# Two gate products ahead of the retention branch, instead of one, in a hybrid retention and gated-linear-attention layer

## The chip, the cores and the metric

The kernel runs on one core of a Trainium2 chip. The metric is the device time of one execution in microseconds (us). A core has a matrix engine (TensorE, in the profile PE for matmuls and PEld for weight loads), VectorE (DVE), ScalarE (ACT), GpSimd (POOL), SyncE (SP, which here only issues DMAs), and 16 DMA engines.

## What is computed

One decoder layer over 528 positions (16 meta tokens ahead of 512 tokens), model width 1024, in float32. One input projection gives the parts of two branches and two merge gates. Cut to what matters here:

```python
u = rms_norm(h, norm_gain)
(rq, rk, rv, rg, gq, gk, gv, gg, glr, m_ret, m_gla) = jnp.split(u @ w_in, points, axis=-1)
o_ret = head_group_norm(retention_chunked(rope(rq), rope(rk) * 256 ** -0.5, rv), ret_norm_gain) * silu(rg)   # 4 heads: 256 q/k, 512 v
o_gla = head_rms_norm(gla_chunked(gq * 128 ** -0.5, gk, gv, log_a), gla_norm_gain) * silu(gg)                # 4 heads: 128 q/k, 256 v
merged = sigmoid(m_ret) * (o_ret @ w_branch_ret) + sigmoid(m_gla) * (o_gla @ w_branch_gla)
out = rms_norm(h + merged @ w_out, final_norm_gain)[:, 16:]
```

The change touches the stage in which `sigmoid(m_gla)`, the gate of the linear-attention branch, is computed beside `o_ret @ w_branch_ret` of a single retention head.

## The kernel before

**Numbers in two parts.** Every float32 operand of a large matmul is split into a high part (a rounded copy made by ScalarE) and a low part (the difference, made by VectorE): `split`, line 153, recorded at line 154. A product is then three matmuls: high by high, low by high, high by low.

**The quad.** A block of a projection (512 columns) is computed by `quad` (line 257) as seven products instead of eight, with sums of weight blocks on VectorE and sums of input blocks prepared beforehand. Its seven products are separated by `yield`. Each product (line 307) is 24 matmuls of 128x256, recorded at line 318. Before its matmuls come the split of its weights (line 302) and, for some, a sum of weight blocks (lines 355, 356, 371, 377). In the gate quad (`adds=False`) four raw weight tiles are loaded by SyncE (line 288); the fifth, x3, is a tile that VectorE fills at line 355 as the second product's step begins. After products come evacuations: a copy on ScalarE (line 334), a sum on VectorE (line 823), and for the gates a scaling on VectorE (line 1137) and a sigmoid on ScalarE (line 1138).

**The gate of linear attention.** `gates_gla(j)` (line 1362) loads what an earlier stage kept in DRAM (tile kg), runs a quad named mg for 512 columns of `m_gla`, multiplies the kept values by the gate (line 1374) and writes them back through GpSimd's queue (line 1131). Its PSUM tiles are mg_a, mg_b and mg_c, its weights mg_w (raw), mg_h and mg_l (parts).

**The retention branch of one head.** `branch` (line 463), called by `ret_branch(h)` (line 1406), multiplies the head's turned output (oh and ol, high and low) by its rows of `w_branch_ret`. It has eight steps, one for each 128 output columns: 12 matmuls of 128x512 (lines 189, 192, 193, in `mm3`), a copy out of PSUM by ScalarE (line 1409, tile mt), and a DMA from GpSimd that adds it to a DRAM tile (line 1131). Steps 1, 3, 5 and 7 first load and split a weight block (br_w, br_h, br_l).

**What the branch needs first.** `ret_attention(h)` ends with `turn` (line 478): transposes on TensorE (line 484, tile ot), then oh on ScalarE (line 491) and ol on VectorE (line 492), eight of each for a head. This runs between the products of the next head's q/k quad (rqk).

**Buffers.** Raw weight tiles share six buffers, weight parts three for high and three for low (`wsplit`, line 251). The temporary tiles of rope, scores and mt share seven. Quads and branches use PSUM pools of four banks each.

**What sets the order.** The program is written as generators. `weave(dense, chain, skip)` (line 204) takes a step of the dense generator, then, from the skip-th on, a step of the chain. `turns` (line 1172) takes one step of each of its generators in rotation until all have ended. TensorE's large products keep the order in which they are written, since the first matmul of each is made to follow the last of the one before (`pin`, line 183). The other engines' queues are put in order by the framework's planner, from its own estimates, when the kernel is built; at run time each engine works through its queue. The loop at line 1443 goes over the four heads. For heads h = 1 and 2 (line 1449) its middle stage is line 1450: the gate quad and the branch of head h - 1 in turns, with rope of head h (`ret_rope`, line 1242) as the chain. Then follow the head's output gate (quad rg) with the scores, and the values (quad rv).

Of the kernel before, what the change touches and what calls it, by code (L numbers as in the profile page):

```python
# [108 lines left out]
def hybrid_kernel(ctx: ExitStack, tc: tile.TileContext, I, out: bass.AP):  # L109
# [43 lines left out]
    def split(hi, lo, src):  # L153
        return nc.scalar.copy(hi, src), nc.vector.tensor_sub(lo, src, hi.bitcast(F32))  # L154
# [49 lines left out]
    def weave(dense, chain, skip=0):  # L204

        for n, _ in enumerate(dense):
            tick()
            if n >= skip:
                next(chain, None)
        for _ in chain:  # L210
            pass

    def every(gen, n, m=1, other=None):

        for i, _ in enumerate(gen):
            yield
            if i % m == m - 1:
                for _ in range(n - m):
                    if other is not None:
                        next(other, None)  # L220
                    yield

    def run(*gens):
        for g in gens:
            yield from g

    def drain(*gens):
        for g in gens:
            for _ in g:
                tick()  # L230
# [4 lines left out]
    def tick():  # L235

        pend[:] = [(n - 1, f) for n, f in pend]
        while pend and pend[0][0] <= 0:
            pend.pop(0)[1]()
# [223 lines left out]
    def branch(src, row0, oh, ol, name, evac, bank=ppt):  # L463
        for q in range(4):
            raw = wraw(f"{name}_{q}_w")
            hi, lo = wsplit([P, 4, 256], f"{name}_{q}")
            nc.sync.dma_start(raw, src[row0:row0 + 4 * P, q * 256:(q + 1) * 256].rearrange("(k p) c -> p k c", p=P))
            split(hi, lo, raw)
            for cc in range(2):
                c = 2 * q + cc  # L470
                ps = bank(f"{name}_p{c}")
                for k in range(4):
                    mm3(ps, hi[:, k, cc * P:(cc + 1) * P], lo[:, k, cc * P:(cc + 1) * P], oh[:, k, :], ol[:, k, :],
                        k == 0, k == 3, True)
                evac(c, ps)
                yield
# [126 lines left out]
    for q in range(4):  # L603
        raw = graw[q]
        hi, lo = wsplit([P, 2, 512], f"gv0_{q}")
        for kk in range(2):
            kh, k = divmod(2 * q + kk, 4)
            g = ng[:, 2 * q + kk:2 * q + kk + 1]
# [520 lines left out]
    def collect(dst, t, first):  # L1129

        nc.gpsimd.dma_start(dst, t, **({} if first else {"accum_op": ALU.add}))


    def gate(dst, p, q, th, n):
        if q is not None:
            total(dst, p, q)
        nc.vector.tensor_mul(dst, p if q is None else dst, rb[:, th, :256].unsqueeze(1).to_broadcast([P, 2, 256]))
        nc.scalar.activation(dst, dst, AF.Sigmoid, scale=(1.0, -1.0)[n])
# [33 lines left out]
    def turns(*gens):  # L1172
        gens = list(gens)
        while gens:
            for g in list(gens):
                try:
                    next(g)
                    yield
                except StopIteration:
                    gens.remove(g)  # L1180
# [21 lines left out]
    def tmp(name):  # L1202
        return rp.tile([P, 2 * HT], F32, tag="tmp", name=name, bufs=7)[:, :512]
# [4 lines left out]
    def rope(t, c, name, prev=None):  # L1208

        def view(m):  # L1210
            return m[:, :t.shape[2] * t.shape[3]].rearrange("p (h c) -> p h c", h=2)

        m = [view(rp.tile([P, 2 * HT], F32, tag="tmp", name=f"{name}_{i}", bufs=7)) for i in range(4)]
        x = nc.vector.tensor_mul(m[0], t[:, 0], c[0])
        if prev is not None:
            after(x, prev)
            after(nc.vector.tensor_mul(m[1], t[:, 1], c[1]), prev)
        else:
            nc.vector.tensor_mul(m[1], t[:, 1], c[1])
        nc.vector.tensor_sub(m[0], m[0], m[1])  # L1220
        yield
        nc.vector.tensor_mul(m[2], t[:, 1], c[0])
        nc.vector.tensor_mul(m[3], t[:, 0], c[1])
        nc.vector.tensor_add(m[2], m[2], m[3])
        yield
        R[name] = m[0], m[2]

    def ret_qk(h):

        q = rp.tile([P, 2, 2, 256], F32, tag="ql", name=f"q{h}")  # L1230
        k = rp.tile([P, 2, 2, HT], F32, tag="kl", name=f"k{h}")
        R["raw", h] = q, k

        def evac(n, th, x, y):
            d = q[:, :, th] if n else k[:, :, th]
            for t in range(2):
                w = d.shape[2]
                total(d[:, t], x[t][:, :w], y if y is None else y[:, t, :w])

        yield from quad((C_RK + h * 256, C_RQ + h * 256), False, f"rqk{h}", evac, wide=True)  # L1240

    def ret_rope(h):
        q, k = R["raw", h]
        yield from rope(k, (cs[:, 0], cs[:, 1]), f"rpk{h}", None if h % 3 else low[1])
        kh = rp.tile([P, 2, 2, HT], F32R, tag="kh", name=f"kh{h}")
        kl = rp.tile([P, 2, 2, HT], F32R, tag="kl", name=f"kl{h}")
        for i, m in enumerate(R[f"rpk{h}"]):
            split(kh[:, i], kl[:, i], m)
        for r in range(4):
            nc.gpsimd.tensor_copy(km[:, :, 32 * r:32 * r + NM].rearrange("p k (h m) -> p k h m", h=2),  # L1250
                                  (kh if r < 3 else kl)[:, :, :, 256:HT].bitcast(F32))
        yield
        yield from rope(q, (cs[:, 0, :, :256], cs[:, 1, :, :256]), f"rpq{h}")
        qh = rp.tile([P, 2, T], F32R, tag="qh", name=f"qh{h}")
        ql = rp.tile([P, 2, T], F32R, tag="ql", name=f"ql{h}")
        R["qk", h] = qh, ql, kh, kl
        for i, m in enumerate(R[f"rpq{h}"]):
            split(qh[:, i].rearrange("p (h c) -> p h c", h=2), ql[:, i].rearrange("p (h c) -> p h c", h=2), m)
        yield

    def ret_g(h):
        sg = rp.tile([P, NTB, 512], F32, tag="sg", name=f"sg{h}")
        R["sg", h] = sg
        yield from quad((C_RG + h * 512, C_RG + h * 512 + 256), True, f"rg{h}", rows_into(sg, AF.Silu),
                        ahead=h % 3 == 0, behind=R.get(("pow", h - 1)))
# [96 lines left out]
    def gates_gla(j):  # L1362

        c = slice(4 * j, 4 * j + 4)
        g = rp.tile([P, 4, T], F32, tag="vl", name=f"mg{j}")
        k = rp.tile([P, 4, T], F32, tag="vh", name=f"kg{j}")
        nc.sync.dma_start(k, kept[:, c, :])

        def evac(n, th, p, q):
            s = slice(2 * n, 2 * n + 2), slice(th * 256, (th + 1) * 256)  # L1370
            gate(g[:, s[0], s[1]], p, q, th, n)

            def later():
                nc.vector.tensor_mul(k[:, s[0], s[1]], k[:, s[0], s[1]], g[:, s[0], s[1]])
                collect(kept[:, c, :][:, s[0], s[1]], k[:, s[0], s[1]], True)

            pend.append((1, later))

        yield from quad((C_MG + j * 512, C_MG + j * 512 + 256), False, f"mg{j}", evac, adds=False)
# [26 lines left out]
    def ret_branch(h):  # L1406
        def evac(c, ps):
            t = tmp(f"mt{h}{c}")
            nc.scalar.copy(t, ps)
            collect(kept2[:, c, :], t, h == 0)  # L1410

        oh, ol = R["o", h]
        yield from branch(I["w_branch_ret"], h * 512, oh, ol, f"br{h}", evac, pat)
# [29 lines left out]
    for h in range(4):  # L1443
        if h == 0:
            drain(ret_qk(h))
        else:
            at = ret_attention(h - 1)
            weave(ret_qk(h), at if h < 3 else islice(at, NTB + 1))
        if h % 3:
            weave(turns(gates_gla(h - 1), ret_branch(h - 1)), ret_rope(h), skip=2)  # L1450
            weave(ret_g(h), ret_scores(h))
            drain(ret_v(h))
        else:
            weave(run(ret_g(h), ret_v(h)), run(every(ret_rope(h), 3, 2, at if h else None), ret_scores(h)))
# [153 lines left out]
```

## Time and profile before

| what | us |
|---|---|
| runs | 764.01, 763.93, 763.68 |
| median | 763.93 |
| profiled execution, span from first to last instruction | 762.2 |
| TensorE busy | 750.4 (98%) |
| VectorE busy | 611.2 (80%) |
| ScalarE busy | 451.2 (59%) |
| GpSimd busy | 133.4 (17%) |

The profile is one execution. Its page has no time beside the span; the runs' median is 1.75 us above it. Times of rows are counted from the span's start. A row of the timeline gives start and duration in us, engine, line, operation, output<-inputs, shapes and a count, and in brackets the idle time of the engine before it with what ended that. "L492" is line 492 of the kernel. Durations of matmuls overlap, since they are pipelined.

### The profile page before, as it was taken

The page shows a single profiled execution, that of the slowest core. Times are in us where ns is not written, and L with a number is a line of the kernel's source. Part 1 is how long each engine was busy: PE and PEld are TensorE (multiplying, and loading weights), DVE is VectorE, ACT ScalarE, POOL GpSimd, SP SyncE. Part 2 cuts the span into 40 slices and gives each one's busy share as a digit, 9 for nine tenths or more (in the row PEclk, how much of TensorE's full clock was granted, in tenths as well). Part 3 has the DMA queues.
Part 4 walks back from the last instruction along what each step waited for, and adds up shares of the span by engine and source line. Part 5 has one row for each costly group of instructions (what it writes and reads, how often), then busy time and mean ns, then how long its engine had stood idle before and what let it go on. Part 6 is the DMA issues. An engine that isn't in the chain of part 4 may idle for free.

```text
span 762.2 us, 14057 instructions
## 1 busy us (share of the span) xinstructions
PE 750.4 (98%) x5595; PEld 701.5 (92%) x5595; DVE 611.2 (80%) x873; ACT 451.2 (59%) x764; POOL 133.4 (17%) x172
## 2 busy tenths in 40 slices
PE   9999999999989999999999999999999999999996
PEld 6799899999989999998889999889999999988996
DVE  6799877689897799778957688876787989775994
ACT  7897584666974465545646455555554756532562
POOL 2211200112231122110330100240002210111142
PEclk9999999999999999999999999999999999999999
DMA  9864321822568973753684563696477357687503
GB/s 301 277 146 106 89 84 45 185 82 70 137 168 229 295 171 91 164 144 119 176 239 125 117 161 111 166 206 154 120 166 159 93 148 193 227 196 199 136 29 111
DMA packets 99995, 116.89 MB, mean 153 GB/s; under 512 B 5717, under 2 KB 90837, under 8 KB 99673
## 3 DMA queue, kind: packets, MB, share of 16 engines
q1 hardware_dynamic: 79896, 88.19, 37.8%
q0 software_dynamic: 19744, 27.27, 19.6%
q8 instruction: 44, 0.72, 0.4%
q10 hardware_dynamic: 288, 0.53, 0.2%
q14 instruction: 23, 0.18, 0.1%
HBM read 104.44 MB, written 11.53 MB: 152 GB/s over the span
## 4 chain that ended last, share of the span: by engine, by line
PE 87%; DVE 9%; issue 2%; ACT 1%; POOL 0%; POOLq 0%; DVEq 0%
PE rv_b L318 6%; PE rg_b L318 6%; PE rqk_b L318 5%; PE rqk_c L318 4%; PE br_p L192 4%; PE br_p L193 3%; PE br_p L189 3%; PE gg_b L318 3%; PE mr_b L318 3%; PE gv_p L640 3%; PE rv_c L318 3%; PE bg_b L318 3%; PE rg_c L318 3%; PE mg_b L318 2%; PE gg_c L318 2%
## 5 line engine op out<-in xcount | busy, mean ns | idle before, releaser
L192 PE MATMUL br_p<-ol,br_h 128*128 128x512 f32 x128 | 50.6, 395 | 1.7 <-DVE ol L492 1.7
L189 PE MATMUL br_p<-oh,br_h 128*128 128x512 f32 x128 | 50.4, 394 | 0.0
L193 PE MATMUL br_p<-oh,br_l 128*128 128x512 f32 x128 | 50.3, 393 | 0.0
L154 ACT CAST rv_h<-rv_w 128x1024 fp32r<-128x1024 f32 x24 | 25.2, 1052 | 26.9 <-DVE rv_w L371 9.6
L154 DVE TENSOR_TENSOR rv_l<-rv_w,rv_h 128x1024 fp32r<-128x1024 f32 x24 | 29.3, 1221 | 9.2 <-ACT rv_h L154 9.2
L154 DVE TENSOR_TENSOR rg_l<-rg_w,rg_h 128x1024 fp32r<-128x1024 f32 x20 | 24.4, 1219 | 8.4 <-ACT rg_h L154 8.4
L192 PEld LDWEIGHTS br_p<-ol,br_h 128*128 128x128 f32 x128 | 24.0, 188 | 7.4 <-DVE ol L492 2.4
L154 ACT CAST br_h<-br_w 128x1024 fp32r<-128x1024 f32 x16 | 16.8, 1050 | 23.4 <-PE br_p L192 9.9
L282 POOL DMA_DIRECT2D rqk_x<-in_w_in_dram x8 | 10.4, 1305 | 109.5 <-DVE vl L154 66.2
L193 PEld LDWEIGHTS br_p<-oh,br_l 128*128 128x128 f32 x128 | 24.0, 188 | 5.5
L154 ACT CAST rg_h<-rg_w 128x1024 fp32r<-128x1024 f32 x20 | 21.0, 1052 | 13.2 <-PE br_p L192 5.0
L189 PEld LDWEIGHTS br_p<-oh,br_h 128*128 128x128 f32 x128 | 24.0, 188 | 5.1 <-ACT oh L491 0.2
L318 PE MATMUL rv_b<-rv_l,fh 128*128 128x256 f32 x96 | 27.1, 282 | 0.1
L318 PE MATMUL rqk_b<-fh,rqk_h 128*128 128x256 f32 (+1 forms) x96 | 27.2, 283 | 0.0
L318 PE MATMUL rqk_b<-fh,rqk_l 128*128 128x256 f32 (+1 forms) x96 | 27.1, 282 | 0.0
L318 PE MATMUL rqk_b<-fl,rqk_h 128*128 128x256 f32 (+1 forms) x96 | 27.1, 282 | 0.0
L154 DVE TENSOR_TENSOR rqk_l<-rqk_w,rqk_h 128x1024 fp32r<-128x1024 f32 x20 | 24.4, 1220 | 3.3 <-ACT rqk_h L154 3.3
L318 PE MATMUL rg_b<-rg_h,fl 128*128 128x256 f32 x96 | 27.0, 281 | 0.0
L318 PE MATMUL rv_b<-rv_h,fl 128*128 128x256 f32 x96 | 27.0, 281 | 0.0
L318 PE MATMUL rg_b<-rg_h,fh 128*128 128x256 f32 x96 | 26.9, 281 | 0.0
L318 PE MATMUL rg_b<-rg_l,fh 128*128 128x256 f32 x96 | 26.9, 281 | 0.0
L318 PE MATMUL rv_b<-rv_h,fh 128*128 128x256 f32 x96 | 26.9, 280 | 0.0
(720 smaller groups left out, 3239.4 us busy)
## 6 DMA issues: line engine op xcount, KB each, us to landing
rv_w<-in_w_in_dram SPq DMA_DIRECT2D x16, 512.0 KB, 4.2
br_w<-in_w_branch_ret_dram SPq DMA_DIRECT2D x16, 512.0 KB, 3.5
rqk_w<-in_w_in_dram SPq DMA_DIRECT2D x12, 512.0 KB, 4.5
rg_w<-in_w_in_dram SPq DMA_DIRECT2D x12, 512.0 KB, 5.4
rqk_x<-in_w_in_dram SPq DMA_DIRECT2D x8, 512.0 KB, 5.3
rqk_x<-in_w_in_dram POOLq DMA_DIRECT2D x8, 512.0 KB, 8.1
rg_x<-in_w_in_dram SPq DMA_DIRECT2D x8, 512.0 KB, 4.2
rg_x<-in_w_in_dram POOLq DMA_DIRECT2D x8, 512.0 KB, 7.7
```

What stands on the lines that cost most here:

```text
L154: return nc.scalar.copy(hi, src), nc.vector.tensor_sub(lo, src, hi.bitcast(F32))
L189: m = nc.tensor.matmul(o, lh, rh, start=first, stop=False)
L192: nc.tensor.matmul(o, lh, rl, start=False, stop=False)
L193: m = nc.tensor.matmul(o, ll, rh, start=False, stop=last)
L282: x = nc.gpsimd.dma_start(t, block(0, 1), accum_op=ALU.add)
L318: m = nc.tensor.matmul(ps[t][:, :n] if wide else ps[t], l, r, start=first and j == 0, stop=kk == 3 and j == 2, skip_group_check=not fresh ...
L640: m = nc.tensor.matmul(pss[t], (al if j == 1 else ah)[t // 2, kh][:, k, c], (lo if j == 2 else hi)[:, kk, :], start=q == kk == j == 0, sto ...
```

## The change

The line that alternates the gate quad and the branch is replaced by two:

```diff
         if h % 3:
-            weave(turns(gates_gla(h - 1), ret_branch(h - 1)), ret_rope(h), skip=2)
+            g = gates_gla(h - 1)
+            weave(run(islice(g, 2), turns(ret_branch(h - 1), g)), ret_rope(h), skip=2)
             weave(ret_g(h), ret_scores(h))
             drain(ret_v(h))
```

`run` chains generators; `islice(g, 2)` takes the first two steps of the gate quad. With g for a gate product and b for a branch step, the order before is g1 b1 g2 b2 g3 b3 g4 b4 g5 b5 g6 b6 g7 b7 b8. After it is g1 g2 b1 g3 b2 g4 b3 g5 b4 g6 b5 g7 b6 b7 b8. The steps of rope still begin with the third step of this sequence, which was g2 and is now b1. Everything else is as it was.

## The prediction

> **What bounds the kernel now.** I read the page's header first, then the waits of TensorE, then the busy time of each engine by stretch, then the timeline of three engines where TensorE waits.
>
> ```profile
> span 762.2 us, 14057 instructions
> PE 750.4 (98%) x5595; PEld 701.5 (92%) x5595; DVE 611.2 (80%) x873; ACT 451.2 (59%) x764; POOL 133.4 (17%) x172
> ```
>
> TensorE is busy for 750.4 of 762.2 us. No reordering can win more than the 11.8 us between, and most of those lie outside the changed stage. The waits of TensorE have one row that belongs to it:
>
> ```profile
> PE br_p L192 <- DVE ol L492: 1.7, 2, 0.9
> ```
>
> Read: matmuls of the retention branch (tile br_p, line 192) waited 1.7 us in all, twice, for VectorE's low half of the turned attention output (ol, line 492). Twice, because the edited line runs for h = 1 and h = 2. The stretches show where (busy us of each engine in a stretch, then the granted clock, DMA share and GB/s):
>
> ```profile
> 341.40:358.80 17.40, 16.49 (x127) 15.48 (x126) 16.99 (x28) 9.15 (x18) 0.55 (x1) 1.00 0.28 91
> 358.80:461.20 102.40, 102.40 (x756) 95.71 (x755) 76.70 (x100) 56.98 (x82) 16.56 (x23) 1.00 0.61 165
> 461.20:478.70 17.50, 16.75 (x129) 15.79 (x128) 17.10 (x28) 9.17 (x18) 0.55 (x1) 1.00 0.27 91
> 478.70:757.00 278.30, 277.12 (x2013) 258.23 (x2011) 221.67 (x310) 146.63 (x229) 55.39 (x69) 1.00 0.60 154
> ```
>
> In the two short stretches VectorE (third busy figure) is full: 16.99 of 17.40 us and 17.10 of 17.50. There TensorE stops, for 17.40 - 16.49 = 0.91 and 0.75 us. Between them TensorE has no idle at all, and behind them 278.30 - 277.12 = 1.18 us, so what is saved there should arrive at the end. The granted clock is 1.00 in all four.
>
> **The stall's true size.** TensorE at head 0 and then at head 1 (start, duration, engine, line, output<-inputs):
>
> ```profile
> 354.61 0.39 PE L189 MATMUL br_p<-oh,br_h 128*128 128x512 f32 x1
> ...
> 356.70 0.50 PE L192 MATMUL br_p<-ol,br_h 128*128 128x512 f32 x1 [0.91 <-DVE ol L492]
> ...
> 358.67 0.28 PE L318 MATMUL mg_a<-xh,mg_h 128*128 128x256 f32 x1
> ...
> 361.53 0.39 PE L189 MATMUL br_p<-oh,br_h 128*128 128x512 f32 x1
> ...
> 364.32 0.28 PE L318 MATMUL mg_b<-fh,mg_h 128*128 128x256 f32 x1
> ```
>
> ```profile
> 474.74 0.39 PE L189 MATMUL br_p<-oh,br_h 128*128 128x512 f32 x1
> ...
> 476.58 0.50 PE L192 MATMUL br_p<-ol,br_h 128*128 128x512 f32 x1 [0.75 <-DVE ol L492]
> ...
> 478.55 0.28 PE L318 MATMUL mg_a<-xh,mg_h 128*128 128x256 f32 x1
> ```
>
> A branch product is 12 matmuls. The second one, undisturbed, occupies 364.32 - 361.53 = 2.79 us. The first takes 358.67 - 354.61 = 4.06 at head 0 and 478.55 - 474.74 = 3.81 at head 1. The excess is 1.27 + 1.02 = **2.29 us**. The idle figures in brackets give only 0.91 + 0.75 = 1.66. I take the starts: the listed durations, 0.39, overlap (12 matmuls in 2.79 us are 0.23 apart), so the matmul before the gap is shown busy for some time in which nothing follows it. The Trainium skill (Perfetto Trace Analysis, section Tensor Engine Instruction (MATMUL, LD_WEIGHTS)) says that a matmul's end in a profile is computed and not observed. By the idle column the time would be 763.93 - 1.66 = 762.3, inside the forecast's own range below; durations of 0.39 at a spacing of 0.23 agree with the skill that the ends are no measure.
>
> **The change, part by part.** It adds and removes no work. TensorE's order of products (g: gate product of 24 matmuls; b: branch product of 12) goes from g1 b1 g2 b2 g3 b3 ... g7 b7 b8 to g1 g2 b1 g3 b2 ... g7 b6 b7 b8.
>
> (1) g2 fills the wait. A g takes 361.53 - 358.67 = 2.86. With g1 ending at 354.61 as now, g2 runs to 357.47, and b1's second k, whose L192 stalled, comes four matmuls later, at 358.4. VectorE, same place:
>
> ```profile
> 351.20 1.21 DVE L154 TENSOR_TENSOR br_l<-br_w,br_h 128x1024 fp32r<-128x1024 f32 x1
> ...
> 353.12 1.21 DVE L154 TENSOR_TENSOR mg_l<-mg_w,mg_h 128x1024 fp32r<-128x1024 f32 x1
> ...
> 355.04 1.21 DVE L377 TENSOR_TENSOR mg_w<-mg_w,mg_w 128x1024 f32<-128x1024 f32 x1
> 356.17 0.86 DVE L492 SCALAR_TENSOR_TENSOR ol<-ot,rgain,oh 128x256 fp32r<-128x256 f32 x2
> 356.96 1.21 DVE L154 TENSOR_TENSOR mg_l<-mg_w,mg_h 128x1024 fp32r<-128x1024 f32 x1
> ...
> 361.80 0.69 DVE L823 TENSOR_TENSOR mg<-mg_a,mg_x 128x512 f32<-128x512 f32 x1 [1.64 <-PE mg_a L318]
> ```
>
> The last ol pair ends at 357.03, and its first instruction, the one that stalled b1, at about 356.65. That leaves 358.4 - 356.65 = 1.75 us in hand. At head 1 the second k would come at 474.74 + 2.86 + 0.93 = 478.53, and the ol it needs was there when the stall ended, at 476.58: 1.95 us in hand. So the stall goes: -2.29 us.
>
> (2) What is late next is g2's own weights. The two mg_l rows are the low halves for g2 and g3. g2's ends at 353.12 + 1.21 = 354.33, and g2 would start at 354.61: 0.28 us to spare if nothing moves. I expect it earlier. In the new program order g2's split stands ahead of br's, so it should take the place that br_l has at 351.20 and br_l the one at 353.12. The buffers allow that:
>
> ```profile
> 347.66 1.04 ACT L154 CAST br_h<-br_w 128x1024 fp32r<-128x1024 f32 x1
> ...
> 351.92 1.06 ACT L154 CAST mg_h<-mg_w 128x1024 fp32r<-128x1024 f32 x1
> ```
>
> There are three split buffers. g2's cast would take the one that br0 takes now at 347.66, and br0 the one free at 351.92. Either way the sum is the same; earlier only adds margin. br_l ending at 354.33 is ahead of b1 at 357.47.
>
> (3) The raw buffers and SyncE's queue. The fifth raw tile of the gate quad (x3, written by VectorE) is now allocated before the first branch weights.
>
> ```profile
> 337.85 0.37 SPq L467 DMA_DIRECT2D br_w<-in_w_branch_ret_dram  x1
> ```
>
> ```profile
> 342.71 1.22 DVE L355 TENSOR_TENSOR mg_x<-mg_w,mg_w 128x1024 f32<-128x1024 f32 x1
> ```
>
> br_w's load starts when a raw is freed at 337.85, and x3 takes the one freed at 342.7. They swap: br_w would load at 342.7. A br_w load lands in 3.4 to 5.6 us:
>
> ```profile
> DMA to landing us min/median/max: 3.4/3.5/5.6
> ```
>
> That is 348.3 at worst, before the cast at about 351.9: hidden, with 3.6 us to spare. Beyond that cover each late microsecond would cost one. L355 may start up to 4.9 us earlier, which relieves the full VectorE; I count nothing for it, because TensorE has no wait left there to win.
>
> (4) Everything after g2. Behind it both orders alternate, b's one g later. g3 starts at 357.47 + 2.79 = 360.26, and its low half is done at 356.96 + 1.21 = 358.17, 2.1 us before. The gate's evacuation (L823, now idle 1.64 us before it) starts some 4 us earlier. The rope steps hang on the count of products, not on their kind, and follow b1 instead of g2. They feed scores that come after the gate and branch stage. Three b's instead of two end the stage, and their weights were split by then; the copies of b's results are 0.59 us of ScalarE against 2.79 of a product:
>
> ```profile
> 358.87 0.59 ACT L1409 COPY mt<-br_p 128x512 f32<-128x512 f32 x1 [1.82 <-PE br_p L193]
> ```
>
> Cost nothing; if a copy were late, it is PSUM banks (four) that would hold TensorE, from the fifth b on.
>
> (5) GpSimd's queue carries the results' accumulating DMAs and two for the next quad, rg. The later of these:
>
> ```profile
> 385.89 1.31 POOL L282 DMA_DIRECT2D rg_x<-in_w_in_dram  x1 [7.97 <-DVE mg L1137]
> ```
>
> ```profile
> DMA to landing us min/median/max: 3.7/7.4/8.4
> ```
>
> It lands by 394.3 at the longest. Six g and seven b behind b1 are 6 x 2.86 + 7 x 2.79 = 36.7 us, so the stage ends at 358.67 + 36.7 = 395.4 now and at 394.1 then, and this tile enters rg's fifth product, four products of 2.86 later. Some 11 us are in hand, and moving b's results (mt) past g's (kg) in the queue shifts it by an issue or two of at most 1.31 us: hidden.
>
> Sum: -2.29 us on the span of 762.2, that is 759.9. The page gives no time beside the span for the profiled execution; the median of the runs, 763.93, is 1.75 above it. Carried over: **761.6 us**. About 0.2% (1.5 us) is what a measurement of this kernel can tell from no change; 2.29 is 0.30%.
>
> **Rivals.** *The wait only moves.* If the planner keeps g2's low half behind br_l and one more filler slips before it, it comes one place later. The places on VectorE are 355.04 - 353.12 = 1.92 apart, so g2 would wait 1.92 - 0.28 = 1.64 us per head, b1 nothing: 2 x 1.64 - 2.29 = +1.0, 764.9 us. Half a place later (an ol pair of 0.86 ahead) costs 2 x 0.58 and leaves -1.1: 762.8. For it: VectorE is full, and its order isn't strictly the program's (L377 of g3 stands before the last ol pair). Against: nothing in the new order asks for it, and the split buffer comes free at 347.66. Both ends count as no change that can be told. That TensorE's order doesn't change at all is no rival: the first matmul of each product is chained to the last of the one before (pin, line 183).
>
> *ol slips behind the gate's evacuation: slower.* ScalarE hands over the last pair of oh, from which ol is made, here:
>
> ```profile
> 354.76 0.86 ACT L491 ACTIVATE oh<-ot,rgain 128x256 fp32r<-128x256 f32 x2 [0.77 <-DVE ol L492]
> ```
>
> mg_a is now complete at 357.5, so its L823 and L1137 (0.69 each) could be queued on VectorE ahead of the last ol pair, with g3's mg_l (1.21) behind them. VectorE would then wait for mg_a until about 357.7 and reach ol at 357.7 + 1.38 + 1.21 = 360.3, its first half done at 360.8, against 358.4 where b1 needs it: a stall of 2.4 us in place of 1.27, and of 1.02 at head 1 if that goes alike: 4.8 - 2.29 = +2.5, 766.4 us. It is slower than before from an ol end of 358.4 + 1.27 = 359.7 on. The Trainium skill (the same page and section) calls VectorE's execution a strict FIFO; by that such an order could not be mended at run time, and the trace agrees where the full VectorE leaves TensorE waiting 0.91 us on an ol whose inputs ScalarE had finished earlier. Against: ol precedes the gates in program order, ScalarE's part of it is done by 354.76 + 0.86 = 355.62, and the evacuation cannot be ready before 357.5, so a planner has ol ready first.
>
> **How the numbers follow.** Full gain, 761.6: 0.62; its own range is 760.9 (with 0.7 of the 1.18 us that TensorE waits in the last stretch going too) to 762.4 (the edge of what can be told). The wait partly or wholly moves, 762.4 to 765.4: 0.27, likeliest 762.8 to 764.2. ol slips, or a similar upset of a later stage, 766.4: 0.11. The range 760.9 to 764.2 leaves out the slower case and the worse part of the middle one. Faster 0.62, same 0.27, slower 0.11.
>
> **What would show it.** Right: the row of br_p waiting for ol is gone; g2's first matmul follows g1 within 0.2 us; b1 takes 2.8 us; g2's mg_l stands before br_l on VectorE; the rg stage starts 1.2 us earlier after head 0 and 2.3 after head 1, and that distance holds to the end. Wrong: a new row of mg_a waiting for mg_l (first rival), of br_p still waiting for ol (second), or the distance shrinking in a later stage, which would say that the rest isn't bound by TensorE.

## The result, and the profile after

| | before | changed |
|---|---|---|
| runs | 5 | 5 |
| median, us | 764.01 | 761.28 |
| lowest to highest, us | 763.68 to 764.66 | 761.03 to 761.82 |
| profiled execution's own time, us | not given | 761.8 |
| its span, us | 762.2 | 760.0 |

The ratio of changed to before is 0.9967, with a 95% interval of 0.9956 to 0.9977: 0.33% faster, about 2.5 us. The forecast was 761.6 us, faster.

The page of the changed kernel begins like this:

```profile
span 760.0 us, 14059 instructions
PE 749.8 (99%) x5595; PEld 701.8 (92%) x5595; DVE 611.4 (80%) x873; ACT 450.8 (59%) x764; POOL 141.9 (19%) x172
```

The matmuls are the same in number (5595) and their busy time is nearly the same, 749.8 against 750.4 us. The span is 2.2 us shorter, so what went is idle time of TensorE. These are the waits that the view of TensorE's waits now lists (engine, tile and line that waited, what it waited for, us in all, times, longest):

```profile
PE bg_b L318 <- DVE bg_l L154: 1.3, 1, 1.3
PE warm_p L574 <- DVE warm L571: 1.2, 1, 1.2
PE bg_b L318 <- ACT bg_x L334: 0.8, 1, 0.8
PE gf L910 <- ACT gon L999: 0.5, 1, 0.5
PE wo_b L318 <- ACT wo_x L334: 0.2, 1, 0.2
PE rv_b L318 <- DVE rv_l L154: 0.2, 1, 0.2
```

The row of br_p waiting for ol is gone, and no row of mg_a, mg_b or mg_c has come in its place. The row of rv_b (0.2 us, in the later stage of the values) is not in the list of before; experiments 1 and 2 have it too, with TensorE's first products in the order of before, so the change is not what brings it. The stretches that hold the changed stage, at head 0 and at head 1 (busy us of PE, PEld, DVE, ACT and POOL, then the granted clock, DMA share and GB/s):

```profile
341.40:394.00 52.60, 52.60 (x354) 48.25 (x353) 44.95 (x64) 29.63 (x45) 16.54 (x19) 1.00 0.64 195
460.00:513.00 53.00, 53.00 (x357) 48.57 (x356) 45.02 (x64) 29.93 (x45) 18.05 (x19) 1.00 0.73 189
```

TensorE is busy for the whole of both. Where the saved time went is read from the chain of the work that ended last. A row is a product of 24 matmuls (start, us, engine, tile, line, matmuls); the chain counts it from the listed end of the matmul before, so these starts lie some 0.2 us behind those of the timeline, in both kernels alike. Four marks of the kernel before, and then the same four of the changed one (a product ahead of the stage, the first rg product after head 0, after head 1, and the output projection):

```profile
211.57 2.85 PE bg_b L318 x24
...
395.33 2.85 PE rg_b L318 x24
...
515.15 2.85 PE rg_b L318 x24
...
735.82 3.34 PE wo_b L318 x24
```

```profile
211.55 2.85 PE bg_b L318 x24
...
394.06 2.85 PE rg_b L318 x24
...
512.92 2.85 PE rg_b L318 x24
...
733.61 3.35 PE wo_b L318 x24
```

Subtract row by row: -0.02, -1.27, -2.23 and -2.21 us, and -2.2 at the end of the span. Nothing was won ahead of the stage, 1.27 at head 0, another 0.96 at head 1, and nothing was given back later. VectorE at head 0 in the changed kernel:

```profile
338.36 1.21 DVE L355 TENSOR_TENSOR mg_x<-mg_w,mg_w 128x1024 f32<-128x1024 f32 x1
...
350.08 1.22 DVE L154 TENSOR_TENSOR mg_l<-mg_w,mg_h 128x1024 fp32r<-128x1024 f32 x1
...
353.92 1.22 DVE L154 TENSOR_TENSOR br_l<-br_w,br_h 128x1024 fp32r<-128x1024 f32 x1
...
356.07 0.88 DVE L492 SCALAR_TENSOR_TENSOR ol<-ot,rgain,oh 128x256 fp32r<-128x256 f32 x2 [0.15 <-ACT oh L491]
```

The sum of line 355 moved 4.35 us earlier (it was at 342.71), since its buffer comes before br_w's now; g2's mg_l is ahead of br_l; and yet the last pair of ol starts only 0.1 us earlier than the 356.17 of before. The bracket says why: it waits for ScalarE's oh, not for a place on VectorE (and that oh, at 355.56, had waited 1.02 us for the ol pair before it). The gain does not come from a faster VectorE, then, but from TensorE asking later.

### The profile page after: what moved, and what is told of

The parts are those of the page before. It is cut to its first block, busy times and chain, and to the rows that moved or that the text cites. A ratio compares the mean times of both kernels' runs of the same rounds, so it can differ in the third digit from the quotient of the medians.

```text
span 760.0 us, 14059 instructions
## 1 busy us (share of the span) xinstructions
PE 749.8 (99%) x5595; PEld 701.8 (92%) x5595; DVE 611.4 (80%) x873; ACT 450.8 (59%) x764; POOL 141.9 (19%) x172
## 4 chain that ended last, share of the span: by engine, by line
PE 91%; DVE 6%; issue 2%; ACT 1%; POOL 0%; POOLq 0%; DVEq 0%
PE rqk_b L318 6%; PE rv_b L318 6%; PE rg_b L318 6%; PE rqk_c L318 5%; PE br_p L189 4%; PE br_p L193 4%; PE br_p L192 4%; PE gg_b L318 3%; PE mr_b L318 3%; PE mg_b L318 3%; PE gv_p L640 3%; PE rv_c L318 3%; PE bg_b L318 3%; PE rg_c L318 3%; PE gg_c L318 2%
## 5 line engine op out<-in xcount | busy, mean ns | idle before, releaser
L154 ACT CAST rqk_h<-rqk_w 128x1024 fp32r<-128x1024 f32 x20 | 21.0, 1052 | 11.6 <-PE rqk_c L318 2.9
L1349 ACT ACTIVATE on<-av,nm,g_r 128x512 f32<-128x512 f32 x16 | 12.5, 780 | 25.4 <-DVE nm L1347 25.4
```

What stands on the lines that cost most here:

```text
L1349: nc.scalar.activation(on, ps, AF.Identity, scale=r, bias=nm)
```

## The experiments

Each was timed in five rounds beside runs of the kernel before on the same chip, in three groups. The kernel before had a median of 763.80 in the first (experiments 1 to 4), 763.92 in the second (5 to 8), 763.68 in the third (9 to 11).

My theory was that only the order on TensorE counts: g2 fills the time in which ol is not there yet. The rivals are in the order of the experiments: that the buffers' new order relieved VectorE, that any product moved ahead would do the same, and that the cover is thinner than I worked out.

**1. Relief of VectorE without the new order.** The kernel before, with the sums of lines 355 and 356 written one step earlier, ahead of b1:

```diff
         ready = prepare(2, w21) if ahead else None
+        if name[:2] == "mg":
+            x3 = wraw(f"{name}_x3")
+            nc.vector.tensor_add(x3, w22, w12)
+            nc.vector.tensor_add(x1, w12, w11)
         yield
-        if not adds:
+        if not adds and name[:2] != "mg":
```

> The order of products is that of before (g1 b1 g2 b2 ...); only the two VectorE sums of the gate quad's raw weights (lines 355 and 356 of before) are written ahead of the first branch step, as they stand in the changed kernel, where they start 4.3 us earlier. Theory A (g2 fills TensorE's wait for ol): the wait stays; ol hangs on ScalarE's oh and ends no more than 0.3 us earlier per head, so 0 to -0.6 us against before, about 763.7. Rival B (the gain is VectorE's relief by these two sums): -2 to -2.3 us, about 761.7.

Measured: 764.73 us, ratio 1.0010 (1.0001 to 1.0019). The row of the waits grew:

```profile
PE br_p L192 <- DVE ol L496: 2.1, 3, 0.9
```

VectorE has the same work and TensorE the same order, so b1 is still held, three times instead of twice. The rival falls: it would have needed some -2 us. My own theory missed as well, by 0.9 us on the slow side, where I had said that nothing or a little would be won. The chain puts 0.38 us of it between the q/k quad ahead of the stage and rg at head 0, and 0.44 at head 1. The sums themselves are not in the way: they are done at 340.62, ten us ahead of the first ol. But VectorE's queue is in another order behind them, and it comes to the split that stands in front of the last two ol pairs before ScalarE has its operand:

```profile
353.34 1.23 DVE L154 TENSOR_TENSOR mg_l<-mg_w,mg_h 128x1024 fp32r<-128x1024 f32 x1 [0.45 <-ACT mg_h L154]
```

In the kernel before VectorE has no idle time in front of that split, and its last ol pair starts at 356.17, not 356.40. The places that the early sums left free did not bring ol sooner.

**2. The lead, but behind b1.** The kernel before with the order g1 b1 g2 g3 b2 g4 and so on:

```diff
-            weave(turns(gates_gla(h - 1), ret_branch(h - 1)), ret_rope(h), skip=2)
+            g, b = gates_gla(h - 1), ret_branch(h - 1)
+            m = run(islice(g, 1), islice(b, 1), islice(g, 2), turns(b, g))
+            weave(m, ret_rope(h), skip=2)
```

> The order is g1 b1 g2 g3 b2 g4 b3 ... g7 b6 b7 b8: the branch falls one more product behind, but only after b1, so everything behind the first pair is as in the changed kernel and b1 still follows g1. Theory A: b1 waits for ol as before (0.9 and 0.75 us shown idle), 0 +- 0.3 us against before. Rival C (the gain comes from the later order: earlier loads for rg, three branch products at the end): -2 us.

Measured: 763.93 us, ratio 1.0001 (0.9992 to 1.0009).

```profile
PE br_p L192 <- DVE ol L492: 1.7, 2, 0.9
```

The wait has the same three numbers as before the change. A lead of two products is worth nothing in itself. What counts is what stands ahead of b1.

**3. No product moved, only the use of ol.** The kernel before, with the first branch product's 12 matmuls so ordered that the four which read ol come last:

```diff
+                if c == 0:
+                    n = 0
+                    for l, r, ks in ((hi, oh, range(4)), (lo, oh, range(4)), (hi, ol, (0, 2, 1, 3))):
+                        for k in ks:
+                            m = nc.tensor.matmul(ps, l[:, k, col], r[:, k, :], start=n == 0, stop=n == 11)
...
```

> The order of products is that of before; in the first branch product alone the 12 matmuls are reordered: the eight that read oh first, then the four that read ol, in the order k = 0, 2, 1, 3. Theory A: the first ol is needed 8 x 0.233 = 1.87 us after b1's start, about when the last pair of ol ends (356.5 for 354.6 + 1.9 to 2.3), so nearly all of the 2.29 us goes: -1.9 to -2.3 us. Rivals B and C, for which the new order of products or its side effects matter: 0 to -0.3 us.

Measured: 762.49 us, ratio 0.9981 (0.9972 to 0.9990), that is -1.3 us where I expected -1.9 to -2.3.

The new wait, and b1 at head 0 by starts, up to the first matmul of g2:

```profile
PE br_p L477 <- ACT oh L501: 0.3, 1, 0.3
```

```profile
354.34 0.39 PE L477 MATMUL br_p<-oh,br_h 128*128 128x512 f32 x1
355.04 0.96 PE L477 MATMUL br_p<-oh,br_h 128*128 128x512 f32 x3 [0.30 <-ACT oh L501]
...
357.70 0.28 PE L318 MATMUL mg_a<-xh,mg_h 128*128 128x256 f32 x1
```

The wait for ol is gone, and another has come that I had left out: with the products of oh ahead, the later parts of oh are wanted sooner, and ScalarE has them no sooner. By starts, b1 took 357.70 - 354.34 = 3.36 us at head 0, against 4.06 before and 2.79 undisturbed: 0.7 us won of 1.27. So moving the use within the product recovers about half. Moving the product recovers all of it, and in the changed kernel no wait for oh is seen.

**4. The change at head 0 alone.**

```diff
-            weave(run(islice(g, 2), turns(ret_branch(h - 1), g)), ret_rope(h), skip=2)
+            m = (run(islice(g, 2), turns(ret_branch(h - 1), g)) if h == 1 else turns(g, ret_branch(h - 1)))
+            weave(m, ret_rope(h), skip=2)
```

> The changed order for head 0, the order of before for head 1. Theory A: head 0's 1.27 us go, head 1's 1.02 stay: -1.2 to -1.3 us, and br_p waits for ol once instead of twice. If the gain lay in something that the two stages share, or in a planner's order of later stages, it would be near 0 or near -2.3 us.

Measured: 762.43 us, ratio 0.9984 (0.9975 to 0.9993): -1.4 us.

```profile
PE br_p L192 <- DVE ol L492: 0.8, 1, 0.8
```

One wait is left, that of head 1. The interval of the runs, -0.5 to -1.9 us, can't part the 1.27 us that starts gave from the 0.91 of the idle column, but the chain can: from a q/k product ahead of the stage (rqk_b) to rg it is 73.20 us in the kernel before (322.13 to 395.33) and 71.94 here (321.73 to 393.67), 1.26 less.

**5. The change without the swap of buffers.** The first branch weights take their buffer and issue their load ahead of g2, so that line 355 stays late (`first_load` makes that tile and that load, and `branch` takes them over):

```diff
...
-            weave(run(islice(g, 2), turns(ret_branch(h - 1), g)), ret_rope(h), skip=2)
+            weave(run(islice(g, 1), first_load(h - 1), islice(g, 1), turns(ret_branch(h - 1), g)), ret_rope(h), skip=2)
```

> The changed order of products, but the load of the first branch weights is written ahead of g2, so that it gets its raw buffer as before and the two VectorE sums (lines 355 and 356) stay where they were before. Theory A: g2 still fills the wait, -2.0 to -2.3 us against before, as the changed kernel. Rival B (VectorE's relief by the two sums is the gain): 0 to -0.5 us.

Measured: 761.54 us, ratio 0.9967 (0.9955 to 0.9979), the same ratio as the change itself. VectorE:

```profile
342.22 1.23 DVE L355 TENSOR_TENSOR mg_x<-mg_w,mg_w 128x1024 f32<-128x1024 f32 x1
```

Line 355 is back within 0.5 us of its old place, and the whole gain is there. With experiment 1 this settles it from both sides: the swap is neither needed for the gain nor enough for it.

**6. One more product ahead.** `islice(g, 3)` in place of `islice(g, 2)`:

```diff
-            weave(run(islice(g, 2), turns(ret_branch(h - 1), g)), ret_rope(h), skip=2)
+            weave(run(islice(g, 3), turns(ret_branch(h - 1), g)), ret_rope(h), skip=2)
```

> The gates go three products ahead instead of two. Theory A: no wait for ol is left at a lead of two, so a third product wins nothing: within 0.3 us of the changed kernel, -2.0 to -2.5 us against before. If lead itself were worth something (earlier loads or evacuations), it would be faster than the changed kernel by 1 us or more; if four branch products in a row at the end hold up TensorE, slower than it.

Measured: 771.63 us, ratio 1.0089 (1.0076 to 1.0102). That was a clear miss. The waits, and the chain at head 0 (start, us, engine, tile, line):

```profile
PE mg_c L318 <- DVE mg_l L154: 5.7, 2, 2.9
```

```profile
374.86 0.58 ACT mt L1409
375.44 0.53 ACT qh L154
376.00 0.69 DVE ql L154
376.69 1.15 DVE mg_l L154
377.88 4.39 PE mg_c L318 x22
```

Read it from the end. g6 waits for the low half of its weights. On VectorE's queue that split stands behind ql, a step of rope; ql needs ScalarE's qh; and qh stands behind the copy of b3's result, where b3 is the product right ahead of g6. Two queues in fixed order tie g6 to the end of b3, and TensorE stops for 2.9 us. This is the prediction's first rival (the wait moves to the gate's weights), with another neighbour in the queue and one product further on. The last row shows a second cost: 22 matmuls in 4.39 us are 0.20 us apart, where 24 in 2.85 are 0.12. More on this in the last section.

**7 and 8. How much cover there is.** Each ol of the second half is computed twice for these heads (the second time with the same value), in the kernel before and in the changed one. That is four more instructions of some 0.43 us (half a pair of 0.86) on VectorE per head, all ahead of b1:

```diff
-                nc.vector.scalar_tensor_tensor(ol[:, k, half * 256:(half + 1) * 256], v, g, h.bitcast(F32),
-                                               op0=ALU.mult, op1=ALU.subtract)
+                for _ in range(2 if half and name in ("ot0", "ot1") else 1):
+                    nc.vector.scalar_tensor_tensor(ol[:, k, half * 256:(half + 1) * 256], v, g, h.bitcast(F32),
+                                                   op0=ALU.mult, op1=ALU.subtract)
```

> The kernel before with the four ol instructions of the second half computed twice for heads 0 and 1: two more pairs of 0.8 us on VectorE ahead of the ol that b1 waits for. Theory A: b1 waits 1.6 us longer per head, +3.2 us (+2.4 to +3.4) against before.

> The changed kernel with the same four ol instructions computed twice; the planner also puts one mg_l (1.2 us) ahead of the last of them. The cover is 2.0 us (ol done at 356.5, needed at 354.75 + 2.85 + 0.93 = 358.5). Theory A: of 1.6 to 2.8 us the cover takes 2.0, so 0 to 0.8 us per head is left: -2.2 to -0.6 us against before. Rival (no cover; VectorE's work costs alike in both orders): +3.2 on the changed kernel, that is +1.0 us against before.

Measured: 768.15 us on the kernel before, ratio 1.0057 (1.0043 to 1.0072), and 762.44 on the changed one, ratio 0.9981 (0.9973 to 0.9990). By the medians the same work costs 4.2 us in the one and about 1 us in the other (762.44 - 763.92 = -1.5, where the change alone has -2.4 to -2.7). The matmul of b1 that was held longest at head 0, in each:

```profile
357.54 0.80 PE L192 MATMUL br_p<-ol,br_h 128*128 128x512 f32 x1 [1.70 <-DVE ol L493]
```

```profile
358.52 0.50 PE L192 MATMUL br_p<-ol,br_h 128*128 128x512 f32 x1 [0.49 <-DVE ol L493]
```

With the old order each delay of ol goes straight onto b1. With the new one about the first 2 us of it are covered, and a rest of 0.49 us shows. The planner also put an mg_l ahead of the last ol pairs in this one, so the delay that was covered is, if anything, larger than the doubling. That ol has cover is shown, and that it is limited too; its size to the tenth of a microsecond is not.

**9. Three products ahead, and rope later.** Experiment 6 with rope begun two steps later:

```diff
-            weave(run(islice(g, 2), turns(ret_branch(h - 1), g)), ret_rope(h), skip=2)
+            weave(run(islice(g, 3), turns(ret_branch(h - 1), g)), ret_rope(h), skip=4)
```

> Three products ahead as in the run that lost 7.7 us, but with rope beginning two steps later (skip=4), so that rope's last split (ql) is queued behind the sixth gate product's low half (mg_l) instead of ahead of it. Theory D (in that run VectorE's queue held mg_l behind ql, which waited for ScalarE behind the copy of b3's result, and TensorE waited 2.9 us per head and then ran at a lower granted clock): the wait for mg_l goes, -2.0 to -2.4 us against before, like the changed kernel. Rival E (a lead of three starves the gate of split buffers, or four branch products in a row hold TensorE up): still slower than before, +5 us or more.

Measured: 770.59 us, ratio 1.0086 (1.0073 to 1.0100), a miss again.

```profile
PE mg_b L318 <- DVE mg_l L154: 4.1, 2, 2.1
...
PE rg_c L318 <- DVE rg_l L154: 0.7, 2, 0.3
...
PE mg_b L318 <- ACT mg_x L334: 0.3, 1, 0.3
```

g6 (mg_c) no longer waits; g7 (mg_b) waits instead, 2.1 us at the longest, again for a split on VectorE. Rope's place decides which product is held. That it decides whether one is held isn't shown, and by this run it does not. By the trace, g7's split was not waiting for an operand or a buffer when it came to run: it starts at 382.10 with no idle time before it, and VectorE had worked without a gap since 376.65, on the gates' evacuation, five steps of rope and ql, all of them queued ahead of it. Why the planner puts it that late, and whether the three split buffers have a part in that, wasn't tried and stays open. The number fits rival E of the expectation (+5 us or more), but neither of the two causes that it names is shown.

**10 and 11. The largest wait that is left.** In the changed kernel the two rows of bg_b make up 2.1 of TensorE's waits. Ahead of them VectorE and GpSimd run side by side:

```profile
218.84 3.30 POOL L1115 TENSOR_TENSOR og1gq<-og1gq,og 128x1024 f32<-128x1024 f32 x1
```

```profile
219.80 3.43 DVE L154 TENSOR_TENSOR gs<-og,gs 128x1024 fp32r<-128x1024 f32 x1
```

The split takes 3.43 us, where splits of this size take 1.22 (mg_l and br_l above), and it ends 1.1 us after GpSimd's sum. Experiment 10 takes the sum of line 1115 to VectorE, four `yield`s later in its generator (the expectations call this two steps); experiment 11 leaves it on GpSimd and writes it at that later place.

```diff
-        nc.gpsimd.tensor_add(a01, a01, a00)
         yield
...
         gform(A22, a11, list(low))
+        nc.vector.tensor_add(a01, a01, a00)
         yield
```

> The changed kernel, and in the earlier stage of the linear-attention branch the sum of line 1115 (128x1024, 3.30 us on GpSimd) goes to VectorE and two steps later. There TensorE waits 0.77 and 1.29 us for bg_x and bg_l, and then runs at a granted clock of 0.50 to 0.87 for some 3 us; a VectorE split that takes 1.22 us elsewhere takes 3.43 beside GpSimd's sum and ends 1.1 us behind it. Theory F (VectorE is shut out while GpSimd's sum runs, and the stall costs the clock as well): bg_l comes 2 us earlier, the stall is at most 0.5 us, the clock stays; -3.0 to -4.1 us against the changed kernel, about 757.5. Rival G (the stretch is the split's own, or VectorE is too full for one more sum of 1.2 us): within 1 us of the changed kernel.

> The changed kernel, and the same sum stays on GpSimd but is issued two steps later. Theory F: the split that was held runs in 1.2 us and another VectorE instruction beside the sum is held instead, where more time is in hand: -1 to -4 us against the changed kernel. Rival G: within 1 us of it, and the split still takes about 3.4 us.

Measured: 759.99 us with the sum on VectorE, ratio 0.9949 (0.9937 to 0.9962), which beats both kernels; 761.61 with the sum later on GpSimd, ratio 0.9971 (0.9960 to 0.9982), which is no more than the change has. In experiment 10 the split runs alone and the waits of the stage shrink:

```profile
220.44 1.22 DVE L154 TENSOR_TENSOR gs<-og,gs 128x1024 fp32r<-128x1024 f32 x1
```

```profile
PE bg_c L318 <- ACT bg_x L334: 0.5, 1, 0.5
...
PE bg_c L318 <- DVE bg_l L154: 0.3, 1, 0.3
```

The mechanism was right and the size was not: the span is 760.0 - 758.2 = 1.8 us shorter than the changed kernel's, and the median 1.6 us below that of experiment 11, where I had expected 3.0 to 4.1. Two marks inside the run, bg_b and the first gate product, say where the rest is:

```profile
212.18 2.85 PE bg_b L318 x24
...
350.10 2.86 PE mg_b L318 x24
```

From bg_b to mg_b it is 137.92 us here and 351.89 - 211.55 = 140.34 in the changed kernel, so the stage gave 2.4 us; 0.6 of it is hidden by a bg_b that came 0.63 us later in this execution. Of 2.1 us of waits, new ones of 0.8 came back, which leaves 1.3. The other 1.1 us is the granted clock, which fell to 0.50 behind these waits in the changed kernel's profiled execution and stayed at 1.00 here:

```profile
227.00:229.00 2.00, 1.44 (x10) 1.24 (x11) 2.00 (x3) 1.18 (x2) 0.00 (x0) 1.00 0.77 272
```

The trace of experiment 2 parts the two. It has the same waits for bg_b, 0.77 and 1.29 us, and its clock stayed at 1.00 behind them (last section). From this bg_b product to the next row of that name in the chain it is 29.73 us in the changed kernel, 28.57 in experiment 2 and 27.32 here: 1.16 us for the clock and 1.25 for the waits. Only the second part is to be had in every execution; the changed kernel loses the first in some of its own.

Experiment 11 does not tell the theories apart: the planner put GpSimd's sum where it had been. It repeats the observation, though: the sum again ran beside a split, which took 3.42 us and ended 1.08 us after it.

## Why the prediction was right

**The bound.** Right. A wait of TensorE in this stage ended up in the total in full: -1.27 and -2.23 us in the chain, -2.2 in the span.

**The size by starts.** Right, and this was the choice that mattered. Starts gave 1.27 + 1.02 = 2.29 us, the idle column 0.91 + 0.75 = 1.66. The chain shows 1.27 + 0.96 = 2.23, and in experiment 4 1.26 for head 0 alone. The Trainium skill (Perfetto Trace Analysis, section Tensor Engine Instruction (MATMUL, LD_WEIGHTS)), by which a matmul's end is computed, agrees with this: the matmul ahead of the gap hid 0.36 us of it at head 0.

**Step 1, the cover.** Right. g2 starts 0.12 us after g1's last matmul, and b1 runs unbroken at both heads. With the first ol of the last pair there at about 356.5 and its use at 358.38, 1.9 us are in hand (1.75 forecast; the 2.0 in experiment 8's expectation took the chain's starts), and experiment 8, which delays ol by more, leaves a wait.

**Step 2, g2's weights.** Right. g2's mg_l moved from 353.12 to 350.08, ahead of the 351.20 that I named.

**Step 3, the buffers.** Right that it counts for nothing (experiments 1 and 5). br_w's load went out at 342.92, where 342.7 was forecast. The remark beside it, that an earlier line 355 relieves VectorE, was too friendly: experiment 1, with the sums early and the products in the order of before, was 0.9 us slower.

**Steps 4 and 5, the later stage and GpSimd's queue.** Right in that no wait of TensorE came of them and the distance holds to the end. The gate's evacuation came 3.3 us earlier (358.54 for 361.80), not some 4. GpSimd's busy time rose from 133.4 to 141.9 us; most of that is the three casts of line 1250, which took 5.63 us at head 0 and 5.32 at head 1, where they took 1.53 and 1.54. The forecast has no such term. The later rg_x of head 0 was issued at 383.70 all the same, ahead of the 385.89 of before, and TensorE waited for none of it.

**The rivals.** Neither happened here. The first one, a wait that moves to the gate's weights, is real one product further: experiment 6 has it, for +7.7 us. My price for it, 1.64 us per head, was far too low there, because the chain through two queues and the clock were not in it. The second, ol behind the gate's evacuation, did not show in any run.

The median came 0.3 us below the forecast. I carried 1.75 us from span to time; the profiled execution of the changed kernel has 1.8, its own time is 761.8, and the median of the runs is 0.5 below that. This is a difference between executions, not a step of the sum: the two runs with a mean granted clock of 0.997 took 761.80 and 761.82 us, the three with 0.998 took 761.03 to 761.28. The profiled one is of the first sort.

## What to carry to other kernels

Where the bound engine waits for a late operand, first measure the stall by the distance of starts against the same product undisturbed, and then put work ahead of it whose own operands are long there, just enough of it to cover the stall. Here one product more took the kernel from 2.5 us faster to 7.7 slower. Before a product is moved, read the queues of the engines that feed it for what stands ahead of its operands, and for what that waits for. A vector operation of three times its usual length is a reason to look at what GpSimd does at that time.

## What the runs showed of the hardware

**A wait can cost more than its length, and does not always.** In experiment 7 the stretches around the wait of 1.70 us:

```profile
356.00:358.00 2.00, 0.46 (x1) 0.46 (x2) 2.00 (x6) 1.08 (x2) 0.00 (x0) 0.80 0.00 0
358.00:360.00 2.00, 2.00 (x6) 1.52 (x6) 2.00 (x3) 0.00 (x0) 0.00 (x0) 0.50 0.00 0
```

The granted clock (third figure from the end) is 0.50 in the two microseconds behind it, and TensorE gets 6 matmuls of a branch product done in 2 us, where 12 take 2.79. Experiment 7's six runs fall into two groups: 767.00, 767.04 and 767.09 us at a mean granted clock of 0.996, and 769.22, 770.01 and 770.21 at 0.991 to 0.993. The trace is of the 769.22. The first group lies within the +2.4 to +3.4 of the expectation, which knew only the waits; the second is above it, and the median of 768.15 lies between the two. The changed kernel shows the same behind its waits of 0.77 and 1.29 us for bg_b, and experiment 6 behind its stop of 2.9:

```profile
225.00:227.00 2.00, 1.45 (x10) 1.45 (x11) 2.00 (x3) 1.92 (x3) 0.00 (x0) 0.87 0.70 223
227.00:229.00 2.00, 2.00 (x11) 2.00 (x10) 2.00 (x4) 0.59 (x1) 0.00 (x0) 0.50 0.79 232
```

```profile
378.00:380.00 2.00, 2.00 (x13) 2.00 (x14) 0.96 (x1) 0.00 (x0) 0.00 (x0) 0.67 1.09 317
```

But the same two waits for bg_b, 0.77 and 1.29 us, left the clock at 1.00 in experiment 2:

```profile
227.00:229.00 2.00, 1.82 (x16) 1.62 (x16) 2.00 (x4) 1.05 (x3) 0.00 (x0) 1.00 0.90 246
```

And experiment 9 has one wait of 2.06 us for mg_l at each head. The product behind it, first at head 0 and then at head 1:

```profile
383.36 2.87 PE mg_b L318 x22
...
504.91 4.38 PE mg_b L318 x22
```

The clock was 1.00 behind the first and 0.50 behind the second, and the second product took 1.51 us longer. So the length of the wait alone does not decide it; what does isn't shown here. The waits of 0.91 and 0.75 us that the change removed left the clock at 1.00. The Trainium skill (TensorE: Matmul & The Clock Gate, section What's actually happening) has the clock halve after an idle window of about 3.4 us; the half is there in these rows, but behind a stop of 1.70 us already.

**VectorE held up by GpSimd.** The split of 3.43 us starts 0.96 us after GpSimd's sum does and ends 1.09 us after the sum's end, which is about the 1.22 us that it takes by itself once the sum is gone from GpSimd (experiment 10). The Trainium skill (SBUF — State Buffer, section SBUF: two separate sides) says that GpSimd and a VectorE operation with two SBUF inputs lock one pair of ports against each other, and that the later one stands still for the whole of the other's instruction. These rows agree with it: 222.14 - 219.80 = 2.34 us of standing still, and then 1.09 of work.
